# 32 bytes more per buffer: the start addresses of weights, xs and h spread over 256 bytes

## The chip, the cores and the metric

The kernel runs on one core of a Trainium2 chip, in one launch. The metric is the device time of that core in microseconds (us), from the first to the last instruction. TensorE (PE in the profile) multiplies, VectorE (DVE), ScalarE (ACT) and GpSimd (POOL) do the elementwise work, SyncE (SP) issues the loads.

## The reference, cut to what matters

Two macaron layers over 512 tokens of width 1024. Each layer is a half-weighted SwiGLU feed-forward, a mixer, and a second feed-forward; a final RMSNorm follows.

```python
def swiglu(x, w_gate, w_up, w_down):
    return (jax.nn.silu(x @ w_gate) * (x @ w_up)) @ w_down

for i in range(DEPTH):                      # DEPTH = 2, D_FF = 2816
    x = x + 0.5 * swiglu(rms_norm(x, ffn_norm[i, 0]), ...)
    hx = rms_norm(x, mix_norm[i])
    x = x + (mixer_ab(hx, ...) if i % 2 == 0 else mixer_cd(hx, ...))
    x = x + 0.5 * swiglu(rms_norm(x, ffn_norm[i, 1]), ...)
return rms_norm(x, final_norm)
```

`mixer_ab` is attention (global beside neighbourhood), `mixer_cd` is a pair of gated convolutions. Everything is float32.

## The kernel before

Activations lie transposed, features on partitions and the 512 tokens along the free axis: `x` is 8 chunks of 128x512. To keep float32 precision with TensorE's fp32r type, each operand is split into a high part (rounded to fp32r) and a low part (the rest), and each product is made as three matmuls (`mm3`, lines 97 to 99): high weights by high x, high weights by low x, low weights by high x. In each of them the weights (128x128) are the stationary operand, loaded by a weight load of its own (PEld in the profile), and x (128x512) is the moving one, streamed through.

The tiles that these matmuls read, all 128 partitions high:

- `raw`: weights as they come from DRAM, 1024 columns, 3 buffers.
- `wh` and `wl`: high and low weights, 512 columns (four blocks of 128), made from `raw` by `split` (lines 117 and 118: a cast on ScalarE, a subtraction on VectorE or GpSimd), 5 buffers each, used in turn. Such a pair is a *piece*; it serves four chunks of the contraction, 12 matmuls. In `mixer_cd` every other piece comes from a second pool, `wx` (`self.extra`), with 5 more buffers each.
- `xs`: the gained high and low part of a chunk of x, side by side, 2x512 columns, 8 buffers, made by `absorb` (lines 126 and 127). It is the moving operand of gate, up and most projections.
- `h`: high and low part of a chunk of the hidden layer, 2x512 columns, 22 buffers in a pool of each feed-forward, made by `gate`. It is the moving operand of the down product.

The mixers' own moving tiles (`y`, `yc`, `yd`, and attention's) are other tiles with buffers of their own.

A feed-forward runs 22 chunks of gate and up (8 chunks of xs each, sums in PSUM tile `psg`), then 8 chunks of down (22 chunks of h each, sums in `psd`). Pieces are made three ahead of their use by `feed`, which `piece` calls. The order of the instructions on each engine is set by the framework's scheduler from the program's order, and in the mixers for PE by hand.

Of the kernel before, what the change touches and what calls it, by code (L numbers as in the profile page):

```python
# [10 lines left out]
F32R = mybir.dt.float32r  # L11
# [5 lines left out]
P = 128  # L17
D = 1024
T = 512
# [8 lines left out]
class Trunk:  # L28
# [27 lines left out]

# [1 line left out]
    def plan(self, units):  # L58
# [16 lines left out]
    def feed(self, upto):  # L75
        nc = self.nc
        while len(self.ready) < min(upto + 1, len(self.pieces)):
            i, c0, c1 = self.pieces[len(self.ready)]
            self.load(i + 1)
            w, r = c1 - c0, self.loaded[i][:, c0:c1]  # L80
            ph, pl = self.wh, self.wl
            if self.extra and len(self.ready) < self.extra_end and len(self.ready) % 2:
                ph = pl = self.extra
            h = ph.tile([P, 512], F32R, tag="wh", name=self.name("wh"))[:, :w]
            l = pl.tile([P, 512], F32R, tag="wl", name=self.name("wl"))[:, :w]
            self.split(h, l, r, self.nc.gpsimd if self.share and len(self.ready) % self.share == 0 else None)
            self.ready.append((h, l))
# [13 lines left out]
    def chunk(self, ps, xs, first=True, last=True):  # L101
        """ps += W[chunk].T @ x over the contraction pieces xs; yields after each."""
        n = len(xs)
        for k, x in enumerate(xs):
            if k % 4 == 0:
                h, l = self.piece()
            s = slice(k % 4 * P, (k % 4 + 1) * P)
            self.mm3(ps, h[:, s], l[:, s], x[:, 0], x[:, 1], first and k == 0, last and k == n - 1)
            yield
# [4 lines left out]

# [1 line left out]
    def split(self, hi, lo, src, eng=None):  # L116
# [3 lines left out]
    def absorb(self, k, gain):  # L120
        """From the residual chunk k: its gained (high, low) pair."""
        nc = self.nc
        g = self.par[:, gain + k : gain + k + 1]
        x = self.x[k]
        xs = self.xsp.tile([P, 2, T], F32R, tag="xs", name=self.name("xs"))
        nc.scalar.activation(xs[:, 0], x, AF.Copy, scale=g)  # L126
        nc.vector.scalar_tensor_tensor(xs[:, 1], x, g, xs[:, 0].bitcast(F32), op0=ALU.mult, op1=ALU.subtract)  # L127
        self.xs[k] = xs
# [11 lines left out]
    def table(self, func, after):  # L140
        """Loads ScalarE's table of func once `after` is there."""
        self.nc.scalar.activation(self.warm, after, func, bias=self.eps)

    def root(self, y, src, scale, after, v=None):
        """y = (src * scale + eps) ** -0.5; then the table of `after`."""
        nc = self.nc
        n = src.shape[1]
        e, v, a = self.t(n), v if v is not None else self.t(n), self.t(n)
        nc.scalar.activation(e, src, AF.Abs_reciprocal_sqrt, bias=self.eps, scale=scale)
        nc.vector.tensor_scalar(v, src, scale, EPS, op0=ALU.mult, op1=ALU.add)  # L150
        if after is not None:
            self.table(after, e[:, :1])
        nc.vector.tensor_tensor(a, e, e, op=ALU.mult)
        nc.vector.scalar_tensor_tensor(a, a, -0.5, v, op0=ALU.mult, op1=ALU.mult)
        nc.vector.scalar_tensor_tensor(y, a, 1.5, e, op0=ALU.add, op1=ALU.mult)  # L155

    def norm(self, after=None):
        """rB[:, t] = rsqrt(mean of x[t]^2 + eps) on all partitions."""
        nc = self.nc
        s = self.fr.tile([P, 2, T], F32R, tag="fr", name=self.name("ss"))  # L160
        self.split(s[:, 0], s[:, 1], self.S)
        ps = self.ps("m")
        nc.tensor.matmul(ps, lhsT=self.ones, rhs=s[:, 0], start=True, stop=False)
        nc.tensor.matmul(ps, lhsT=self.ones, rhs=s[:, 1], start=False, stop=True)
        self.rB = self.rbp.tile([P, T], F32, tag="rB", name=self.name("rB"))
        self.root(self.rB, ps, 1.0 / D, after)
# [13 lines left out]

# [1 line left out]
    def ffn(self, gain, natural=False, start=False):  # L182
# [41 lines left out]
    def gate(self, hp, pg, pu):  # L224
        nc = self.nc
        g, s, h = self.t(), self.t(), self.t()
        nc.vector.tensor_tensor(g, pg, self.rB, op=ALU.mult)  # L227
        nc.scalar.activation(s, g, AF.Silu)  # L228
        nc.vector.tensor_tensor(s, s, self.rB, op=ALU.mult)  # L229
        nc.vector.tensor_tensor(h, pu, s, op=ALU.mult)  # L230
        hh = hp.tile([P, 2, T], F32R, tag="h", name=self.name("h"))
        self.split(hh[:, 0], hh[:, 1], h)
        return hh

    def finish(self, hs):
        """The last down projection and the final norm; the last chunk by halves of the tokens."""
        nc = self.nc
        gf = lambda k: self.par[:, 48 + k : 49 + k]
        for d in range(NK - 1):
            ps = self.ps("d")  # L240
# [6 lines left out]
        pieces = []  # L247
# [53 lines left out]

# [1 line left out]
    def column(self, k, n=1):  # L303
        return self.par[:, k : k + n]

    def rope(self, src):
        """src [feature pairs on partitions, tokens] -> rotated, in place of a new tile."""
        nc = self.nc
# [65 lines left out]
    def row_scales(self):  # L374
        """Per token, on its partition: r, and for each head of A the scale of its scores."""
        nc = self.nc
        ps = self.ps("m")
        for t in range(4):
            nc.tensor.transpose(ps[:, t * P : (t + 1) * P], self.rB[:, t * P : (t + 1) * P], self.ident)
        self.rc = self.abc.tile([P, 4], F32, tag="rc", name="rc")  # L380
        nc.vector.tensor_copy(self.rc, ps.rearrange("p (t q) -> p t q", q=P)[:, :, 0])
# [23 lines left out]
    def values(self, half):  # L405
        """Value columns of `half`, tokens on partitions; yields after each contraction step."""
        nc = self.nc
# [60 lines left out]
    def fill(self, n):  # L468
        """n steps of the fillers; those of A's output wait for its heads."""
        done = 0  # L470
# [6 lines left out]

    # units: (kind, pair, e, tile); "a": 128 queries x 512 keys, "b": 128 queries x 256 keys
    def scores(self, u):
# [41 lines left out]
    def turn(self, u, pr):  # L521
        """Probabilities of a unit to keys-on-partitions, split into the group's tiles."""
        nc = self.nc
# [14 lines left out]
    def mix(self, u, pt):  # L538
        """Values by a finished group's probabilities. The values' high and low parts stand side
        by side, so each pass leaves two sums, one of them on the head's own partitions."""  # L540
        nc = self.nc
# [29 lines left out]

    def ab_start(self):
        """Keys, queries and first values, their small chains a step behind the products."""
        nc = self.nc

# [102 lines left out]

# [1 line left out]
    def padded(self):  # L680
# [6 lines left out]
    def conv_vector(self, j, u, k0=0):  # L687
        """Taps k0.. of 31 over the padded chunk u on VectorE, one per step, the sums in PSUM;
        alone, with two sums in turn, else in turn with the next chunk."""
        nc = self.nc  # L690
# [19 lines left out]
    def conv_spare(self, j, u, k1=31):  # L710
        """Taps ..k1 on ScalarE (products) and GpSimd (sums)."""
        nc = self.nc
# [21 lines left out]
    def conv_step(self, n):  # L734
        """n steps of the convs on VectorE: the first alone, the others two at a time."""
        while n > 0 and self.convs:
# [7 lines left out]
    def total(self, src):  # L744
        """Sum of src over the partitions, on all of them, in PSUM."""
        ps = self.ps("m")
# [63 lines left out]
    def c_out(self):  # L810
        """The short conv's half of the output product; six of its sums stay open in PSUM."""
        nc = self.nc
# [40 lines left out]
    def mixer_cd(self, gain):  # L853
        nc = self.nc
        with self.tc.tile_pool(name="cdp", bufs=1) as self.cdp, self.tc.tile_pool(name="wx", bufs=5) as self.extra:
# [22 lines left out]
            with self.tc.manual_schedule(engines={mybir.EngineType.PE}):  # L878
# [5 lines left out]
                self.share = 0  # L884
                # the first sums side by side: the chunks of y come one by one
                k = 3
# [63 lines left out]
def cols(v):  # L950
    """[..., n * 128] -> [128, ... * n]"""
    return v.reshape(-1, P).T


def bias_table(rpb):
    """[head, query in tile, tile, key]: the bias of each pair in reach, -1e30 elsewhere.
    Tokens run down the grid's columns: token = col * 8 + row."""
    q = np.arange(512).reshape(4, P, 1)
# [9 lines left out]
def constants():  # L968
    """identity, blocks of ones by head, signed swap of pairs, head selectors, cos, sin."""
    f = np.float32  # L970
# [57 lines left out]
```

## Time and profile before

| what | value |
|---|---|
| device time, median of 2 runs | 1896.6 us (1895.97 and 1897.22) |
| profiled execution, span | 1896.4 us |
| PE busy | 1862.0 us, 98% |
| weight loads (PEld) busy | 1525.5 us, 80% |
| VectorE, ScalarE, GpSimd busy | 51%, 40%, 20% |
| HBM traffic | 94 GB/s over the span |
| TensorE's mean granted clock | 0.992 of full speed |

The profiled execution's own time is its span; the two timed runs lie 0.4 us below and 0.8 us above it, so nothing has to be added around it. A matmul's duration in the profile runs from its start to its modelled end and overlaps the next one's, so what it costs in a stream is read from the distance between the starts of two matmuls that follow each other, here called the *interval*.

### The profile page before, as it was taken

How to read it: one execution, taken by the hardware profiler on the slowest of the kernel's cores; microseconds unless marked ns; L12 is line 12 of the kernel's file. 1: busy time of each engine (PE TensorE's matmuls, PEld its weight loads, DVE VectorE, ACT ScalarE, POOL GpSimd, SP SyncE). 2: the span in 40 equal slices, each digit the busy share in tenths (PEclk: the TensorE clock that was granted, in tenths of full speed). 3: DMA queues.
4: the chain of work that ended last, by engine and by line, in shares of the span. 5: the costliest groups of instructions: out<-in, count | busy, mean ns of one | idle time of the engine just before them, and what ended most of it. 6: DMA issues, size and time to landing. Idle time of an engine off the chain costs nothing.

```text
span 1896.4 us, 22618 instructions
## 1 busy us (share of the span) xinstructions
PE 1862.0 (98%) x8382; PEld 1525.5 (80%) x8382; DVE 973.7 (51%) x1534; ACT 764.3 (40%) x1336; POOL 381.0 (20%) x358
## 2 busy tenths in 40 slices
PE   8999999989999999999999999999998999999997
PEld 7888888878877888888888888888886788888886
DVE  6544433387865744443334444422599755444333
ACT  5333333357755533333333333333464543333332
POOL 0000000045332222222222222222399100000000
PEclk9999999999999999999999999999999899999999
DMA  4232233312122323223323222233322222222332
GB/s 169 100 100 93 95 92 97 118 55 91 40 95 67 125 97 100 98 90 92 93 95 102 98 100 100 86 98 96 122 90 67 87 82 99 100 97 90 92 96 71
DMA packets 56576, 179.00 MB, mean 94 GB/s; under 512 B 6161, under 2 KB 8465, under 8 KB 56465
## 3 DMA queue, kind: packets, MB, share of 16 engines
q1 hardware_dynamic: 55888, 176.71, 28.8%
q8 instruction: 66, 1.08, 0.2%
q10 hardware_dynamic: 576, 0.84, 0.1%
q14 instruction: 46, 0.37, 0.1%
HBM read 175.43 MB, written 2.10 MB: 94 GB/s over the span
## 4 chain that ended last, share of the span: by engine, by line
PE 95%; DVE 3%; issue 1%; ACT 0%; POOL 0%; DMA 0%; DVEq 0%; POOLq 0%; ACTq 0%
PE psg L97 20%; PE psg L98 20%; PE psg L99 19%; PE psd L97 11%; PE psd L98 11%; PE psd L99 11%; PE psm L528 1%; PE psg L558 1%; PE psg L557 1%; PE psg L489 0%; PE psg L490 0%; DVE psm L700 0%; DVE wl L118 0%; DVE x L280 0%; DMA raw<-in_gate 0%
## 5 line engine op out<-in xcount | busy, mean ns | idle before, releaser
L117 ACT CAST wh<-raw 128x512 fp32r<-128x512 f32 (+1 forms) x662 | 400.2, 607 | 905.1 <-PE psg L98 549.8
L97 PE MATMUL psg<-xs,wh 128*128 128x512 f32 x1592 | 619.6, 390 | 6.1 <-ACT xs L126 6.1
L98 PE MATMUL psg<-xs,wh 128*128 128x512 f32 x1592 | 620.6, 390 | 0.0
L99 PE MATMUL psg<-xs,wl 128*128 128x512 f32 x1592 | 620.1, 390 | 0.0
L118 DVE TENSOR_TENSOR wl<-raw,wh 128x512 fp32r<-128x512 f32 (+1 forms) x469 | 326.7, 697 | 454.5 <-ACT wh L117 451.4
L118 POOL TENSOR_TENSOR wl<-raw,wh 128x512 fp32r<-128x512 f32 (+1 forms) x193 | 250.8, 1300 | 634.4 <-ACT wh L117 624.2
L97 PEld LDWEIGHTS psg<-xs,wh 128*128 128x128 f32 x1592 | 299.5, 188 | 69.0 <-ACT xs L126 6.1
L98 PEld LDWEIGHTS psg<-xs,wh 128*128 128x128 f32 x1592 | 299.4, 188 | 62.6 <-DVE xs L127 0.5
L99 PEld LDWEIGHTS psg<-xs,wl 128*128 128x128 f32 x1592 | 299.4, 188 | 62.4
L99 PE MATMUL psd<-h,wl 128*128 128x512 f32 (+1 forms) x726 | 282.0, 388 | 0.0
L98 PE MATMUL psd<-h,wh 128*128 128x512 f32 (+1 forms) x726 | 282.0, 388 | 0.0
L97 PE MATMUL psd<-h,wh 128*128 128x512 f32 (+1 forms) x726 | 281.8, 388 | 0.0
L99 PEld LDWEIGHTS psd<-h,wl 128*128 128x128 f32 x726 | 136.3, 188 | 31.2
L97 PEld LDWEIGHTS psd<-h,wh 128*128 128x128 f32 x726 | 136.3, 188 | 31.2
L98 PEld LDWEIGHTS psd<-h,wh 128*128 128x128 f32 x726 | 136.3, 188 | 31.1
L230 DVE TENSOR_TENSOR t<-psg,t 128x512 f32<-128x512 f32 x87 | 60.1, 691 | 124.4 <-PE psg L99 124.1
L227 DVE TENSOR_TENSOR t<-psg,rB 128x512 f32<-128x512 f32 x87 | 60.1, 691 | 121.4 <-PE psg L99 121.4
L229 DVE TENSOR_TENSOR t<-t,rB 128x512 f32<-128x512 f32 x88 | 72.7, 826 | 34.4 <-ACT t L228 30.7
L118 DVE TENSOR_TENSOR h<-t,h 128x512 fp32r<-128x512 f32 x88 | 73.0, 830 | 32.5 <-ACT h L117 28.8
L280 POOL TENSOR_TENSOR x<-x,t 128x256 f32<-128x256 f32 x4 | 3.2, 829 | 396.3 <-DVE t L155 396.3
L626 POOL MEMSET pb<- 128x384 f32 x2 | 0.8, 418 | 371.3 <-PE psd L99 371.3
L228 ACT ACTIVATE t<-t 128x512 f32<-128x512 f32 x88 | 55.6, 632 | 25.9 <-DVE t L227 25.8
(238 smaller groups left out, 1635.3 us busy)
## 6 DMA issues: line engine op xcount, KB each, us to landing
raw<-in_gate SPq DMA_DIRECT2D x84, 512.0 KB, 3.2
raw<-in_up SPq DMA_DIRECT2D x84, 512.0 KB, 3.2
raw<-in_down SPq DMA_DIRECT2D x64, 448.0 KB, 3.3
raw<-in_down SPq DMA_DIRECT2D x32, 512.0 KB, 3.5
raw<-in_cdin SPq DMA_DIRECT2D x18, 512.0 KB, 3.2
raw<-in_abqk SPq DMA_DIRECT2D x13, 512.0 KB, 3.3
raw<-in_about SPq DMA_DIRECT2D x16, 256.0 KB, 2.7
bias<-in_bias SPq DMA_DIRECT2D x8, 512.0 KB, 3.3
```

The source lines that it names most:

```text
L97: mm(ps, lhsT=aH, rhs=bH, start=first, stop=False)
L98: mm(ps, lhsT=aH, rhs=bL, start=False, stop=False)
L99: mm(ps, lhsT=aL, rhs=bH, start=False, stop=last)
L117: self.nc.scalar.copy(hi, src)
L118: (eng or self.nc.vector).tensor_tensor(lo, src, hi.bitcast(F32), op=ALU.subtract)
L227: nc.vector.tensor_tensor(g, pg, self.rB, op=ALU.mult)
L228: nc.scalar.activation(s, g, AF.Silu)
L229: nc.vector.tensor_tensor(s, s, self.rB, op=ALU.mult)
L230: nc.vector.tensor_tensor(h, pu, s, op=ALU.mult)
L528: nc.tensor.transpose(ps[:, i * P : (i + 1) * P], pr[:, i * P : (i + 1) * P], self.ident)
L557: nc.tensor.matmul(ps, lhsT=w, rhs=pt[0][:, p0:p1], start=first, stop=False)
L558: nc.tensor.matmul(ps, lhsT=w, rhs=pt[1][:, p0:p1], start=False, stop=last)
```

## The change

Three kinds of tile get 8 float32 columns (32 bytes) more per partition than they use: `wh` and `wl` (both pools), `xs`, and `h`. The views that the instructions use stay as they were. The diff also empties comments and docstrings (lines stay where they are); its core:

```diff
@@ feed
-            h = ph.tile([P, 512], F32R, tag="wh", name=self.name("wh"))[:, :w]
-            l = pl.tile([P, 512], F32R, tag="wl", name=self.name("wl"))[:, :w]
+            h = ph.tile([P, 520], F32R, tag="wh", name=self.name("wh"))[:, :w]
+            l = pl.tile([P, 520], F32R, tag="wl", name=self.name("wl"))[:, :w]
@@ absorb
-        xs = self.xsp.tile([P, 2, T], F32R, tag="xs", name=self.name("xs"))
+        xs = self.xsp.tile([P, 2 * T + 8], F32R, tag="xs", name=self.name("xs"))[:, : 2 * T].rearrange("p (a t) -> p a t", a=2)
@@ gate
-        hh = hp.tile([P, 2, T], F32R, tag="h", name=self.name("h"))
+        hh = hp.tile([P, 2 * T + 8], F32R, tag="h", name=self.name("h"))[:, : 2 * T].rearrange("p (a t) -> p a t", a=2)
```

On all five engines the instructions stand in the same order before and after, with the same buffers and the same waits; only addresses differ. The start of each buffer within a partition, modulo 256 bytes, as the two programs allocate them (a block of weights begins a multiple of 512 bytes into its buffer, a low part 2048 bytes into its own, so these offsets hold for every operand that a matmul reads):

| buffers | before | after, in the order of the buffers |
|---|---|---|
| `xs` (8) | 128 | 128, 160, 192, 224, 0, 32, 64, 96 |
| `wh` (5) | 128 | 128, 160, 192, 224, 0 |
| `wl` (5) | 128 | 32, 64, 96, 128, 160 |
| `wh` in `wx` (5) | 64 | 128, 160, 192, 224, 0 |
| `wl` in `wx` (5) | 64 | 32, 64, 96, 128, 160 |
| `h` (22) | 0 | 64, 96, 128, ... in steps of 32 |
| `raw` (3) | 128 | 128 |
| `t`, `S`, `rB` | 128 | 192 |
| `y` of attention | 0 | 64 |
| `yc`, `yd` of the convolutions (split) | 64 | 128 |

Below, the *distance* of a matmul is the start of its moving operand less the start of the weights that are loaded while it runs (those of the next matmul), modulo 256 bytes.

## Rows read from the trace of the kernel before

**Rows 1.** Page, parts 1 and 2: busy time, and the span in 40 slices.
```profile
PE 1862.0 (98%) x8382; PEld 1525.5 (80%) x8382; DVE 973.7 (51%) x1534; ACT 764.3 (40%) x1336; POOL 381.0 (20%) x358
...
PE   8999999989999999999999999999998999999997
...
PEclk9999999999999999999999999999999899999999
```

**Rows 2.** Page, part 4: the chain that ended last, by engine and line.
```profile
PE 95%; DVE 3%; issue 1%; ACT 0%; POOL 0%; DMA 0%; DVEq 0%; POOLq 0%; ACTq 0%
PE psg L97 20%; PE psg L98 20%; PE psg L99 19%; PE psd L97 11%; PE psd L98 11%; PE psd L99 11%; PE psm L528 1%; PE psg L558 1%; PE psg L557 1%; PE psg L489 0%; PE psg L490 0%; DVE psm L700 0%; DVE wl L118 0%; DVE x L280 0%; DMA raw<-in_gate 0%
```

**Rows 3.** Groups by line and shape: matmuls of line 97.
```profile
L97 PE MATMUL psg<-xs,wh 128*128 128x512 f32 x1592 | 619.6, 390 | 6.1 <-ACT xs L126 6.1
...
L97 PE MATMUL psd<-h,wh 128*128 128x512 f32 x682 | 269.4, 395 | 0.0
...
L97 PE MATMUL psd<-xs,wh 128*128 128x512 f32 x80 | 35.1, 438 | 1.7 <-DVE t L433 1.7
```

**Rows 4.** Timeline of PE, gate and up: start, duration, then engine and operation.
```profile
1604.75 0.39 PE L98 MATMUL psg<-xs,wh 128*128 128x512 f32 x1
1604.97 0.39 PE L99 MATMUL psg<-xs,wl 128*128 128x512 f32 x1
...
1649.17 0.39 PE L99 MATMUL psg<-xs,wl 128*128 128x512 f32 x1
```

**Rows 5.** Timeline of PE, a down product.
```profile
1802.70 0.40 PE L99 MATMUL psd<-h,wl 128*128 128x512 f32 x1
1802.94 0.39 PE L97 MATMUL psd<-h,wh 128*128 128x512 f32 x1
...
1848.43 0.40 PE L97 MATMUL psd<-h,wh 128*128 128x512 f32 x1
```

**Rows 6.** Timeline of PE, output product of the convolutions.
```profile
1490.54 0.39 PE L97 MATMUL psg<-yc,wh 128*128 128x512 f32 x1
...
1492.58 0.40 PE L97 MATMUL psd<-yc,wh 128*128 128x512 f32 x1
1492.82 0.39 PE L98 MATMUL psd<-yc,wh 128*128 128x512 f32 x1
...
1495.15 0.39 PE L99 MATMUL psd<-yc,wl 128*128 128x512 f32 x1
...
1496.30 0.40 PE L98 MATMUL psd<-yc,wh 128*128 128x512 f32 x1
...
1496.77 0.39 PE L97 MATMUL psd<-yc,wh 128*128 128x512 f32 x1
...
1498.13 0.40 PE L97 MATMUL psg<-yd,wh 128*128 128x512 f32 x1
```

**Rows 7.** Timeline of PE, input projection of the convolutions, one piece from `wx`.
```profile
1408.72 0.39 PE L97 MATMUL psg<-xs,wh 128*128 128x512 f32 x1
...
1411.47 0.39 PE L97 MATMUL psg<-xs,wh 128*128 128x512 f32 x1
```

**Rows 8.** Stretches: bounds, length, busy PE, PEld, DVE, ACT, POOL, granted clock, DMA.
```profile
640.00:870.00 230.00, 230.00 (x1015) 190.34 (x1015) 102.39 (x132) 80.80 (x130) 54.30 (x42) 1.00 0.29 96
...
260.00:360.00 100.00, 100.00 (x430) 80.43 (x430) 38.26 (x59) 31.43 (x53) 0.00 (x0) 1.00 0.33 97
```

**Rows 9.** Waits of the weight split: total us, times, longest.
```profile
ACT wh L117 <- PE psg L98: 549.8, 339, 3.9
DVE wl L118 <- ACT wh L117: 451.4, 298, 5.2
```

**Rows 10.** Cast of the weights (min/median/max ns): in the convolutions, then in gate and up.
```profile
L117 ACT CAST wh<-raw x16: 600/604/622, 1389.6 to 1437.3; 128x512 fp32r<-128x512 f32 x16
...
L117 ACT CAST wh<-raw x52: 621/622/622, 1599.8 to 1738.5; 128x512 fp32r<-128x512 f32 x52
```

**Rows 11.** Page, part 5: all casts of weights.
```profile
L117 ACT CAST wh<-raw 128x512 fp32r<-128x512 f32 (+1 forms) x662 | 400.2, 607 | 905.1 <-PE psg L98 549.8
```

## The prediction

> **What bounds the kernel now.** I read the page first: PE is busy for 98% of the span and at 9 tenths or more in 36 of 40 slices [rows 1], and the chain of waits that ended last is 95% PE, almost all of it the three matmuls of `mm3` [rows 2]. So the time is a count of matmuls times their interval, and a change that moves no instruction can act only through that interval, or through a slower split that comes late. The groups give the counts: 1592 matmuls of each of the three lines with xs into `psg`, 80 of each with xs into `psd`, 682 of each with h at full width [rows 3]. That is 3 x 1672 = 5016 intervals behind xs and 3 x 682 = 2046 behind h.
>
> The timeline gives the intervals. In gate and up, 196 of them lie between the first and the last row shown: (1649.17 - 1604.75) / 196 = 226.6 ns [rows 4]. In down, again 196: (1848.43 - 1802.70) / 196 = 233.3 ns [rows 5]. [...] What the table of addresses says of them: xs and its weights both begin at 128 modulo 256 (distance 0), h begins at 0 and its weights at 128 (distance 128).
>
> Whether the address is what counts is told by a place where it changes and the moving tile doesn't. In the output product of the convolutions every other piece comes from `wx`, so yc (at 64) meets weights at 64 for 12 matmuls and then weights at 128 for 12. With weights at 64 (distance 0), 9 intervals from 1490.54 to 1492.58: 2.04 / 9 = 226.7 ns. With weights at 128 (distance 192), 11 from 1492.58 to 1495.15: 2.57 / 11 = 233.6 ns. Back at 64, 6 from 1496.77 to 1498.13: 1.36 / 6 = 226.7 ns [rows 6]. The PSUM tile isn't the cause, since the last two of these are both `psd`. One more distance: xs at 128 with weights at 64 (distance 64), 12 intervals from 1408.72 to 1411.47, 2.75 / 12 = 229.2 ns [rows 7]. So the price by distance is 226.7 (0), 229.2 (64), 233.3 (128), 233.6 (192).
>
> **The change, part by part.** *xs and its weights.* Today nearly all of these sit at distance 0, the cheapest of the four that the trace shows. Eight places for xs against five for `wh` and five for `wl` put about an eighth of the intervals at each of the eight distances 0, 32, ..., 224. The odd multiples of 32 don't occur before; I take them as lying among their neighbours, so the mean by distance is (226.7 + 229.2 + 233.3 + 233.6) / 4 = 230.7 ns. There is a second part: after a change of distance the stream takes a few matmuls to settle. After the step back to distance 0 the 5 intervals from 1495.15 to 1496.30 take 1.15 / 5 = 230 ns, before 226.7 is reached [rows 6]. With the change the distance moves at almost every matmul, between `wh` and `wl` and from one chunk to the next, so the stream never settles; against that, a single matmul at a dear distance may not reach its full price either. I add 0.8, between nothing and the 3.3 seen: 231.5 ns. The cost is 5016 x (231.5 - 226.7) = 24.1 us, and none of it is hidden, as PE has no gap there to give.
>
> *h and its weights.* They leave distance 128 for the same mixture: 2046 x (231.5 - 233.3) = -3.7 us.
>
> *Bounds of both.* From below, every interval comes to 226.7: nothing for xs, -6.6 x 2046 = -13.5 us for h. From above, every interval is as long as the longest single step of the alternating stretches, 0.24 us between neighbouring rows against a mean of 0.2333 [rows 5, 6]; taken as 237 ns that is 10.3 x 5016 + 3.7 x 2046 = 59 us. I take 231.5 because it is nearest to the mixture of rows, and both ends go into the range.
>
> *y, yc, yd and attention's tiles.* Their own length doesn't change, but their weights now spread, and yc and yd met two distances in turn before. Some 400 matmuls, at 226.7 to 233.6 before and in the same span after: 0, with 400 x 6.9 = 2.8 us either way.
>
> *The split and the other elementwise work.* Its instructions write to starts that are multiples of 32 instead of 64 or 128. The nearest row is the cast in the convolutions, where half of the outputs start at 64 and half at 128: 600 to 622 ns, against 621 to 622 with all of them at 128 [rows 10]. No loss shows. ScalarE's cast waited 549.8 us in all for PE to free a buffer, and VectorE another 451.4 us for the cast [rows 9], so a split that grew by a few per cent would stay under that cover; if all of it showed on PE, 2% of the 400.2 us of all casts of weights [rows 11] would be 8 us. I take 0. The buffers' count, the loads and their sizes are unchanged.
>
> **The sum.** +24.1 - 3.7 = +20.4 us on the profiled execution's own 1896.4, which is within 0.2 us of the median of the runs: **1917 us**, 1.1% slower. That is under the 2% that a measurement of this kernel can tell from no change.
>
> **The rivals.** *Nothing happens: 1896 us.* The address would have to stand in for something else, say the second pool's place high in SBUF or the h pool's. For it: the h stretch and the gate stretch differ in more than the address, and the convolutions' rows are short. Against it: yc reads at 226.7 from `wx`, high in SBUF, and at 233.6 from the ordinary pool, while xs does the opposite, 229.2 and 226.7 [rows 4, 6, 7]. No fixed price of a pool gives both; a distance does.
> [...]
>
> *Faster: the 226.7 is itself a collision.* [...] If two streams that begin in the same place of every 256 bytes are what costs this, then spreading them apart removes some of it wherever the distance isn't 0. [...] It decides from a mean of (5016 x 226.7 + 2046 x 233.3) / 7062 = 228.6 ns downwards, in effect when some of the four unseen distances are much cheaper than the seen ones. Against it: distances 64, 128 and 192 are all dearer than 0. A mild form, in which the mixture comes to no more than 226.7, gives 1896.4 - 13.5 = 1883 us.
> [...]
>
> *Clearly slower: the stream never settles.* If the settling rather than the distance is what costs, and every change of distance brings the long step of an alternating pair without the short one, the mean comes to 235 ns: 8.3 x 5016 + 1.7 x 2046 = 45 us, 1942 us. It passes the 2% line (1934.5 us) from a mean of 234.0 ns on, 5.4 above 228.6. For it: the distance changes at nearly every matmul after the change. Against it: in the rows the long step is always followed by a short one.
>
> **How the numbers follow.** The forecast (mean interval 229.5 to 233.5, 1903 to 1931 us) gets 0.56; nothing happens, 0.10; faster, 0.14, two thirds of it in the mild form near 1883 and 0.05 below 1858.7 us (2%); the stream never settles, 0.20, of which 0.14 lies above 1934.5 us. The range, 1889 to 1942 us, leaves out the strong form of the faster rival, part of the mild one and the upper end of the slow one, together about 2 in 10. From the same cases: faster by over 2% 0.05, within 2% 0.81, slower by over 2% 0.14.
>
> **What would show it.** In the profile after, the mean interval of a stretch of gate and up should be near 231.5 ns instead of 226.6, with no period, and that of a down product about the same instead of 233.3; the two products should have become alike. PE's busy share and the chain should stay as they are, and the granted clock at 1.00. The forecast is wrong if gate and up keep 226.6 (the address isn't it), if both fall under 228.6 (the faster rival), or if they go to 235 and above; and wrong in its reason if PE shows gaps behind the weight split, since then an elementwise engine and not the interval made the difference.

## The result, and the profile after

The changed kernel takes 1916.66 us (1915.64 and 1917.69) against 1896.6 before: a ratio of 1.0105, 95% interval 1.0086 to 1.0125, so 0.9 to 1.3% slower. The profiled execution is the one of 1915.64 us; its span is 1913.9, so about 1.7 us lie outside the span. Every run here of which both are recorded takes 1.7 to 1.9 us longer than its span, those of the kernel before included (1891.77 and 1889.9 us, for one). The span of 1896.4 before should therefore not be read as that execution's time, as "Time and profile before" has it; by these runs it took about 1898 us, an estimate. From span to span the change costs 17.5 us, from median to median 20.1.

The page after, parts 1, 2 and 4, answers to [rows 1] and [rows 2]:

```profile
PE 1882.2 (98%) x8382; PEld 1525.1 (80%) x8382; DVE 970.3 (51%) x1534; ACT 764.2 (40%) x1336; POOL 381.4 (20%) x358
...
PE   8999999999999999999999999999999999999997
...
PEclk9999999999999999999999999999999999999999
...
PE 96%; DVE 3%; issue 1%; ACT 0%; POOL 0%; DMA 0%; DVEq 0%; SPq 0%; POOLq 0%; ACTq 0%
```

The same instructions, the same share of PE, nearly the same mean clock (0.992 and 0.993); weight loads, ScalarE and GpSimd are as busy as before to within 0.4 us, VectorE 3.4 us less. Only PE's busy time has grown, by 20.2 us. Nothing waits anew: the matmuls themselves come further apart. The timeline of PE in the kernel after, first in gate and up, then in a down product, answers to [rows 4] and [rows 5]; in each, 196 intervals lie between the first and the last row shown:

```profile
699.78 0.39 PE L99 MATMUL psg<-xs,wl 128*128 128x512 f32 x1
...
745.21 0.40 PE L97 MATMUL psg<-xs,wh 128*128 128x512 f32 x1
```

```profile
289.63 0.40 PE L97 MATMUL psd<-h,wh 128*128 128x512 f32 x1
...
335.14 0.39 PE L98 MATMUL psd<-h,wh 128*128 128x512 f32 x1
```

Gate and up: (745.21 - 699.78) / 196 = 231.8 ns, before 226.6. Down: (335.14 - 289.63) / 196 = 232.2 ns, before 233.3. The two products have become alike.

Neither the granted clock nor a gap set the two products apart before. [rows 8] show 1.00 and a PE that is busy all the time, in other stretches of the same two products. For the stretches that the prediction read, the view says the same (length, busy PE, then the other engines, granted clock, DMA), gate and up first:

```profile
1604.75:1649.17 44.42, 44.42 (x197) 36.79 (x196) 21.42 (x33) 15.38 (x25) 0.00 (x0) 1.00 0.28 95
1802.70:1848.43 45.73, 45.73 (x197) 36.79 (x196) 15.05 (x25) 14.61 (x24) 0.00 (x0) 1.00 0.33 94
```

and for the two stretches of the kernel after:

```profile
699.78:745.21 45.43, 45.43 (x198) 36.80 (x196) 19.54 (x25) 15.14 (x25) 10.39 (x8) 1.00 0.28 93
289.63:335.14 45.51, 45.51 (x198) 36.81 (x196) 17.51 (x27) 14.27 (x24) 0.00 (x0) 1.00 0.33 95
```

Where the 17.5 us lie is told by the matmul of each norm (line 163), which stands once in every sublayer. Its starts in the timeline of PE, kernel before:

```profile
25.82 0.39 PE L163 MATMUL psm<-ss,ones 128*128 128x512 f32 x1
377.50 0.39 PE L163 MATMUL psm<-ss,ones 128*128 128x512 f32 x1
635.75 0.39 PE L163 MATMUL psm<-ss,ones 128*128 128x512 f32 x1
998.77 0.39 PE L163 MATMUL psm<-ss,ones 128*128 128x512 f32 x1
1361.82 0.39 PE L163 MATMUL psm<-ss,ones 128*128 128x512 f32 x1
1532.89 0.39 PE L163 MATMUL psm<-ss,ones 128*128 128x512 f32 x1
```

The same rows, kernel after:

```profile
25.28 0.39 PE L163 MATMUL psm<-ss,ones 128*128 128x512 f32 x1
381.50 0.40 PE L163 MATMUL psm<-ss,ones 128*128 128x512 f32 x1
640.41 0.40 PE L163 MATMUL psm<-ss,ones 128*128 128x512 f32 x1
1008.21 0.40 PE L163 MATMUL psm<-ss,ones 128*128 128x512 f32 x1
1376.09 0.39 PE L163 MATMUL psm<-ss,ones 128*128 128x512 f32 x1
1545.71 0.40 PE L163 MATMUL psm<-ss,ones 128*128 128x512 f32 x1
```

Differences of neighbouring rows, before and after: first feed-forward 351.7 and 356.2, attention 258.25 and 258.91, second feed-forward 363.0 and 367.8, third 363.1 and 367.9, convolutions 171.1 and 169.6, and the last feed-forward up to the end of the span 363.5 and 368.2. The four feed-forwards lose 4.5, 4.8, 4.8 and 4.7 us, 18.8 together. That is what the intervals give: 1056 matmuls with xs and 528 with h in one of them (at full width 462 in the last), 1056 x 5.2 - 528 x 1.1 = 4.9. The convolutions, whose 480 matmuls with xs should have lost about 2 us (252 x 5.2, and 228 with weights from `wx`, which had 229.2 before [rows 7], x 2.6), are 1.5 us shorter. What PE waited for there, from 1390 to 1530 us (total, times, longest), kernel before:

```profile
PE psd L97 <- ACT yc L117: 5.6, 3, 3.4
PE psd L98 <- DVE yc L118: 2.8, 2, 1.6
```

and kernel after:

```profile
PE psd L97 <- ACT yc L117: 4.1, 2, 3.4
PE psd L98 <- DVE yc L118: 1.6, 1, 1.6
```

PE waits for the elementwise chain that makes yc, 2.7 us less than before. Two things lie in this. The stage up to the place where the granted clock falls, and the stretch that it then stays at 0.50, kernel before:

```profile
1361.82:1465.83 104.01, 100.94 (x441) 82.34 (x439) 102.41 (x132) 59.15 (x95) 89.64 (x68) 1.00 0.26 86
1465.83:1479.48 13.65, 8.32 (x17) 5.50 (x18) 8.57 (x12) 2.90 (x5) 3.75 (x3) 0.50 0.30 97
```

and kernel after:

```profile
1376.09:1480.73 104.64, 102.58 (x441) 82.45 (x439) 100.57 (x133) 59.30 (x95) 90.33 (x68) 1.00 0.27 88
1480.73:1490.97 10.24, 6.63 (x13) 4.20 (x14) 6.89 (x11) 2.89 (x5) 2.55 (x2) 0.50 0.26 89
```

Up to the fall PE works 1.6 us more and idles 1.0 us less: there the slower matmuls do lie partly under the work on yc. The rest is the stretch at a granted clock of 0.50, 3.4 us shorter with 1.7 us less of idle PE in it, against 1.3 us more from there to the end of the stage (53.4 and 54.7 us). The shorter stretch at 0.50 need not come from the slower matmuls: xs_256_longer below, with the intervals of the kernel before, has 10.24 us of it too, and 169.2 us for this stage. Why it differs between executions is not shown.

### The profile page after: what moved, and what is told of

The parts are those of the page before. It is cut to its first block, busy times and chain, and to the rows that moved or that the text cites. A ratio compares the mean times of both kernels' runs of the same rounds, so it can differ in the third digit from the quotient of the medians.

```text
span 1913.9 us, 22618 instructions
## 1 busy us (share of the span) xinstructions
PE 1882.2 (98%) x8382; PEld 1525.1 (80%) x8382; DVE 970.3 (51%) x1534; ACT 764.2 (40%) x1336; POOL 381.4 (20%) x358
## 4 chain that ended last, share of the span: by engine, by line
PE 96%; DVE 3%; issue 1%; ACT 0%; POOL 0%; DMA 0%; DVEq 0%; SPq 0%; POOLq 0%; ACTq 0%
PE psg L97 20%; PE psg L98 20%; PE psg L99 20%; PE psd L97 11%; PE psd L99 11%; PE psd L98 11%; PE psm L528 1%; PE psg L558 1%; PE psg L557 1%; PE psg L489 0%; PE psg L490 0%; DVE psm L700 0%; DVE wl L118 0%; DVE x L280 0%; DMA x<-in_x 0%
## 5 line engine op out<-in xcount | busy, mean ns | idle before, releaser
L97 PE MATMUL psg<-xs,wh 128*128 128x512 f32 x1592 | 626.5, 394 | 6.4 <-ACT xs L126 6.4
L98 PE MATMUL psg<-xs,wh 128*128 128x512 f32 x1592 | 628.2, 395 | 0.0
L99 PE MATMUL psg<-xs,wl 128*128 128x512 f32 x1592 | 627.3, 394 | 0.0
L118 DVE TENSOR_TENSOR h<-t,h 128x512 fp32r<-128x512 f32 x88 | 73.0, 830 | 32.7 <-ACT h L117 28.9
```

The costliest lines, as they stand in the source:

```text
L97: mm(ps, lhsT=aH, rhs=bH, start=first, stop=False)
L98: mm(ps, lhsT=aH, rhs=bL, start=False, stop=False)
L99: mm(ps, lhsT=aL, rhs=bH, start=False, stop=last)
L118: (eng or self.nc.vector).tensor_tensor(lo, src, hi.bitcast(F32), op=ALU.subtract)
```

## The experiments

The theory: the interval is set by the *distance*, as defined with the change, and 0 is the cheap one; spreading the starts took gate and up away from it. Rivals: the moving tile's own start, the tile's length or place, and, in the other direction, an unseen distance cheaper than 0. All intervals below are read as above: 196 intervals, from about 700 us in gate and up and from about 290 us in down. None of these kernels leaves out or moves an instruction; all have the same waits, and only addresses differ. Inserted lines move the three matmuls to lines 98 to 100 or 99 to 101.

**h brought to distance 0 (h_zero).** Nothing is longer; 128 unused bytes stand ahead of the pools that are opened stage by stage, so the mixers' own tiles and `wx` move too.

```diff
+        pool("gap2", 1).tile([P, 32], F32, tag="gap2", name="gap2")
         self.psum = pool("psum", 1, space=bass.MemoryType.PSUM)
```

> No tile is longer; 128 unused bytes stand ahead of the stage pools, so h begins at 128 like its weights. Distance theory: down falls from 233.3 to 226.7 ns an interval, 2046 x -6.6 = -13.5 us, 1883 us. Rival that the interval belongs to the h pool or to the down product itself: 1896 to 1897 us.

Measured: 1881.31 us (1877.97 to 1882.72), ratio 0.9915, 95% interval 0.9899 to 0.9932. The timeline of its down product:

```profile
289.82 0.39 PE L98 MATMUL psd<-h,wh 128*128 128x512 f32 x1
...
334.25 0.39 PE L99 MATMUL psd<-h,wh 128*128 128x512 f32 x1
```

(334.25 - 289.82) / 196 = 226.7 ns, from 233.3. The same instructions, tiles and lengths, 128 bytes further on: the down product isn't slow by itself, and neither is its pool. In the profile the four feed-forwards, in which only h has moved, take 13.3 us less together (3.5, 3.5, 3.4 and 2.9), where 2046 intervals were to give 13.5. This is faster than both kernels of the comparison.

**One part at a time (weights_only, xs_only, h_only).** Each of the three diffs of the change alone.

> Only the weight buffers are 32 bytes longer; xs stays at 128, h at 0. Distance theory: gate and up go to about 232 ns, down to about 232, 1896.4 + 5016 x 5.3 - 2046 x 1.3 = 1920 us. Rival that the moving operand's own start sets the interval: both intervals as before, 1896 us.

> Only xs is longer; weights stay at 128, so the distance is constant over the three matmuls of a chunk and changes from chunk to chunk. If the settled prices hold (226.7, 229.2, 233.3, 233.6 at 0, 64, 128, 192): 230.7 ns, 1916 us. If the stream needs longer than three matmuls to settle: about 232 ns, 1923 us. Down stays at 233.3.

> Only h is longer. Gate and up stay at 226.6; down goes to 230.7 (settled prices, -5 us, 1891 us) or to about 232 (unsettled, -2.7 us, 1894 us). Rival that longer tiles cost by themselves: down slower than 233.3, over 1896 us.

Measured, one run each beside a median of 1896.64 for the kernel before: weights_only 1915.59 us, intervals 232.0 (gate and up) and 231.1 (down); xs_only 1919.66 us, 232.5 and 232.3; h_only 1895.41 us, 226.7 and 232.6. With xs left at 128 and only its weights spread, gate and up slow down as much as after the whole change, so the moving operand's own start isn't what counts. Either side alone costs nearly everything, and the parts don't add: once one of the two is spread, spreading the other changes little. h_only shows that a longer h costs nothing by itself and that a spread gains 0.7 ns on distance 128 (232.6 for 233.3). Two misses: the down product of xs_only was to stay at 233.3 and has 232.3, at the same constant distance of 128; and that of weights_only, at 231.1, is lower than forecast. Its expectation has h at 0, but ten weight buffers that are each 32 bytes longer stand ahead of h and move it by 320, to 64. The timeline of xs_only's down product:

```profile
289.70 0.40 PE L98 MATMUL psd<-h,wh 128*128 128x512 f32 x1
...
335.24 0.40 PE L99 MATMUL psd<-h,wl 128*128 128x512 f32 x1
```

**The constant distances (six kernels).** Tiles of the old lengths; gaps of n and m float32 columns ahead of the weights and ahead of the stage pools hold xs and h each at one distance, two prices per kernel. Each was run once.

```diff
+        pool("gap1", 1).tile([P, n], F32, tag="gap1", name="gap1")
         self.raw = pool("raw", 3)
...
+        pool("gap2", 1).tile([P, m], F32, tag="gap2", name="gap2")
         self.psum = pool("psum", 1, space=bass.MemoryType.PSUM)
```

n and m are 56 and 56 (d32_h96), 40 and 8 (d96_h160), 24 and 24 (d160_h224), 8 and 40 (d224_h32), 48 and 16 (d64_h192), 64 and 96 (d256_h256).

> Tiles of the old lengths; unused bytes ahead of the weights and of the stage pools put xs at a constant distance of 32 from its weights and h at a constant 96. Steady distances, never seen before. If the price rises smoothly from 0: xs about 228 ns, h about 231. If an odd multiple of 32 is cheaper (the collision rival): under 226.7. If only distance 0 is cheap: both about 233.

> Constant distances: xs 96, h 160. The price must belong to the distance and not to the tile: xs at 96 here equals h at 96 in the run before, within 0.5 ns. By interpolation 231 and 233 ns.

> Constant distances: xs 160, h 224. xs at 160 equals h at 160 of the run before. By interpolation 233 and 230 ns; under 226.7 only by the collision rival.

> Constant distances: xs 224, h 32. Each equals the other tile's price at the same distance in the earlier runs. If the settled prices at all eight distances average near 230.7 and the changed kernel has 232, the rest is the settling.

> Constant distances: xs 64, h 192, the two that the kernel before shows only over 12 matmuls at a time. If every distance but 0 costs the same once it is constant: both near 233.3 ns, about 1926 us. If the short stretches gave the steady price: xs 229.2, h 233.6, 1909 us.

> Constant distance of 256 bytes modulo 512 for xs and h. If the pattern repeats every 256 bytes: both 226.7 ns, 1881 to 1884 us, as with distance 0. If it repeats at 512 or more: both near 233.3 ns, 1930 us.

| kernel | time, us | distance of xs: interval, ns | distance of h: interval, ns |
|---|---|---|---|
| before | 1896.6 | 0: 226.6 | 128: 233.3 |
| d32_h96 | 1924.34 | 32: 233.3 | 96: 233.3 |
| d96_h160 | 1926.46 | 96: 233.4 | 160: 234.3 |
| d160_h224 | 1928.21 | 160: 234.3 | 224: 233.4 |
| d224_h32 | 1924.62 | 224: 233.3 | 32: 233.4 |
| d64_h192 | 1903.51 | 64: 228.9 | 192: 233.4 |
| d256_h256 | 1882.87 | 256: 226.7 | 256: 226.7 |

The rows behind three of these, gate and up each, in the order d32_h96, d160_h224, d64_h192:

```profile
699.62 0.40 PE L99 MATMUL psg<-xs,wh 128*128 128x512 f32 x1
...
745.35 0.40 PE L100 MATMUL psg<-xs,wh 128*128 128x512 f32 x1
```

```profile
699.68 0.39 PE L99 MATMUL psg<-xs,wh 128*128 128x512 f32 x1
...
745.60 0.40 PE L100 MATMUL psg<-xs,wh 128*128 128x512 f32 x1
```

```profile
699.80 0.39 PE L101 MATMUL psg<-xs,wl 128*128 128x512 f32 x1
...
744.66 0.39 PE L99 MATMUL psg<-xs,wh 128*128 128x512 f32 x1
```

Where a distance was held by both tiles (32, 96, 160, 224), the prices agree to 0.1 ns: the distance carries the price, not the tile. The pattern repeats at 256 bytes, since 256 costs what 0 costs, 226.7 ns. No distance that was tried is cheaper than 0, which ends the rival that a collision at 0 could be spread away. And all distances but 0 and 64 are about equally dear: there is no slope between 0 and 128 on which 32 would lie, and d32_h96 missed its smooth alternative of 228 by 5 ns. d64_h192 gives 228.9 and 233.4 ns for the 229.2 and 233.6 of [rows 6] and [rows 7]: stretches of 12 matmuls had told the steady price.

**Longer, but by 256 bytes (xs_256_longer).** In `absorb`, before's `[P, 2, T]` becomes `[P, 2 * T + 64]`, with the same view of it as in the change.

```diff
-        xs = self.xsp.tile([P, 2, T], ...)
+        xs = self.xsp.tile([P, 2 * T + 64], ...)[:, : 2 * T].rearrange("p (a t) -> p a t", a=2)
```

> xs is 256 bytes longer instead of 32, so its buffers are moved as much or more but still begin at 128 modulo 256. Distance theory: 226.6 in gate and up, 233.3 in down, 1896 us. Rival that a longer tile with a gap costs by itself: gate and up near 232, 1923 us.

Measured: 1891.86 us beside before's 1894.74 to 1899.1, intervals 226.7 and 233.4, as before. Length and gap cost nothing; the start modulo 256 does. This single run lies under those of before that stand beside it, but not under all: beside h_zero, one run of the kernel before took 1891.77 us. The profile says where the difference lies: the four feed-forwards take the same 351.7, 363.0, 363.1 and 363.5 us as before, and attention 254.3 instead of 258.3, with the granted clock at 1.00 over the stage instead of 0.98. Attention in the kernel before:

```profile
377.50:635.75 258.25, 248.91 (x1311) 203.37 (x1310) 192.87 (x429) 162.09 (x354) 99.63 (x122) 0.98 0.23 76
```

and in xs_256_longer:

```profile
376.99:631.26 254.27, 244.91 (x1312) 199.58 (x1310) 192.03 (x429) 161.96 (x354) 100.92 (x122) 1.00 0.23 77
```

**Distance 0 in the convolutions too (all_zero).** h_zero, and `cu` (a tile of the convolutions) is given 576 columns instead of 514, so that the pools behind it begin at 128 as well.

```diff
-        u = self.cdp.tile([P, 514], F32, tag="cu", name=self.name("cu"), bufs=2)
+        u = self.cdp.tile([P, 576], F32, tag="cu", name=self.name("cu"), bufs=2)
```

> As the run with h at distance 0, and the convolutions' tiles also moved, so that the second weight pool, yc and yd begin at 128 too: distance 0 everywhere but in attention. 229 intervals of xs by 6 ns and some 90 of yc and yd by 2 to 3: 1.5 to 2 us less than that run's 1881.3, about 1879.5 us; the difference to it is too small for the measurement, so the intervals decide.

Measured: 1882.43 us (1882.15 to 1882.88), ratio 0.9927, 95% interval 0.9911 to 0.9944; no better than h_zero. The intervals, which the expectation names as the judge, did fall. Twelve matmuls with xs and weights from `wx` in h_zero, at distance 192,

```profile
1407.98 0.40 PE L98 MATMUL psg<-xs,wh 128*128 128x512 f32 x1
...
1410.78 0.39 PE L98 MATMUL psg<-xs,wh 128*128 128x512 f32 x1
```

and in all_zero, at 0:

```profile
1406.08 0.39 PE L98 MATMUL psg<-xs,wh 128*128 128x512 f32 x1
...
1408.80 0.39 PE L98 MATMUL psg<-xs,wh 128*128 128x512 f32 x1
```

That is 2.80 / 12 = 233.3 and 2.72 / 12 = 226.7 ns, 1.5 us over 228 such intervals. The norm's matmul at both ends of the convolutions, in h_zero

```profile
1349.33 0.39 PE L164 MATMUL psm<-ss,ones 128*128 128x512 f32 x1
1518.59 0.39 PE L164 MATMUL psm<-ss,ones 128*128 128x512 f32 x1
```

and in all_zero:

```profile
1348.50 0.39 PE L164 MATMUL psm<-ss,ones 128*128 128x512 f32 x1
1519.78 0.39 PE L164 MATMUL psm<-ss,ones 128*128 128x512 f32 x1
```

169.3 and 171.3 us: this stage, the only one that the longer `cu` changes, became 2.0 us longer. The stretch at a granted clock of 0.50 in it, h_zero:

```profile
1454.32:1464.56 10.24, 6.27 (x12) 3.89 (x13) 7.26 (x11) 2.90 (x5) 2.54 (x2) 0.50 0.29 98
```

and all_zero:

```profile
1449.95:1467.02 17.07, 10.16 (x20) 6.11 (x21) 12.15 (x17) 4.55 (x8) 7.36 (x6) 0.50 0.27 93
```

The granted clock is at 0.50 for 6.8 us more (17.07 for 10.24), and PE waits 8.9 us for yc instead of 6.8. So the 1.5 us that the matmuls gave are outweighed; what comes first, the wait or the clock, is not shown. The chain of waits (shares from 1340 to 1480 us, h_zero) has much besides PE in this stage:

```profile
by line: POOL yd L721 24.0%; issue 11.6%; PE psg L99 10.9%; PE psg L100 10.8%; PE psg L98 10.8%; POOL wl L119 7.1%; DVE psm L701 5.1%; DVE wl L119 2.7%; DVE yc L119 2.0%; PE psd L98 1.8%; PE psd L99 1.8%; POOL cc L798 1.4%; PE psd L100 1.4%
```

GpSimd's sum of the convolution is the longest single line there, and PE's lines together have 37.5%. The forecast of 1.5 to 2 us less counted matmuls where they only partly set the end.

## Why the prediction came out right, point by point

*That the interval counts and the address sets it* was right. PE's share and the chain stayed as they were, the instructions too, the clock in both products as well, and the two products became alike, at 231.8 and 232.2 ns for 231.5. h_zero is the clean proof, as 128 bytes of nothing move 2046 intervals by 6.6 ns, which makes 13.5 us (13.3 in the profile's feed-forwards), and the time from 1896.6 to 1881.3, where 1883 was expected.

*The price by distance* had a wrong middle. The step "I take them as lying among their neighbours" put the four unseen distances at a mean of 230.7 with the seen ones; held constant, they cost 233.3, 233.4, 234.3 and 233.3. The mean of the eight constant prices is (226.7 + 233.3 + 228.9 + 233.4 + 233.3 + 234.3 + 233.4 + 233.3) / 8 = 232.1 ns.

*The settling* was the second wrong step, the other way. I added 0.8 ns for a stream that never settles; against 232.1 the changed kernel's 231.8 and 232.2 leave nothing to add. A mean taken 1.4 ns too low and an addition 0.8 ns too high partly cancelled in 231.5, which is luck. The reading behind the addition was also short: in [rows 6] the stream is back at 226.7 only from 1496.77 on, 7 intervals after 1495.15, which average 1.62 / 7 = 231 ns. That the mixture costs the mean of the constant prices must not be read as each matmul paying its own price: taking all starts of full-width matmuls with xs from the trace after and sorting the intervals under 300 ns by distance, the 613 at distance 0 average 231.0 and the 608 at distance 160 average 231.5, though constant they cost 226.7 and 234.3. In a mixture the price is one of the mixture, 231.1 to 232.6 ns in the four kernels that have one. Nor is the mean of the constant prices exact: for the down product of weights_only, h at 64 and the weights at their ten places, it would be 232.5 ns, and 231.1 was measured.

*The sum.* xs: 5016 x (231.8 - 226.6) = +26.1 us where +24.1 was forecast. h: 2046 x (232.2 - 233.3) = -2.3 where -3.7 was forecast. That is 23.8, and the span grew by 17.5. (5016 at 226.6 is itself a little too much, since 228 of them were at distance 64.) "None of it is hidden" failed in the convolutions, where 480 of the 5016 intervals lie: up to the fall of the clock 1.0 of 1.6 us was taken back by less idle time of PE, which waits for yc there. The stretch at a granted clock of 0.50, 3.4 us shorter, did the rest, and the stage became 1.5 us shorter instead of about 2 longer; of the clock in that stage the prediction has no term. Attention, whose 312 matmuls with xs should have lost 1.6 us, lost 0.7. The start of the kernel was 0.5 us earlier. So 1917 for 1916.66 is closer than the reasoning was: from span to span +20.4 was forecast and 17.5 came, and the 1.8 us between span and time, taken as 0, lie the other way. The constant distances show the same shortfall: the span of d160_h224 should be 5016 x 7.7 + 2046 x 0.1 = 39 us longer than before and is 30.0 longer: 31.2 in the feed-forwards (32.7 by their intervals), and 1.2 less in the mixers and at the start.

*The rivals.* "Nothing happens" is ruled out by the interval itself: 226.7 against 233.3 ns in h_zero and the kernel before, with the same tiles, the same count and nothing changed for h but its start. Why a different start costs 6.6 ns is not shown. "Faster" is ruled out at the steps of 32 bytes that were tried, none of which is under 226.6. No run shows its strong form, which the range leaves out and which has 0.05 below 1858.7 us: the shortest run of all took 1877.97 us (h_zero). "The stream never settles" at 235 isn't seen: the mixtures stay under 233.

*The split* cost nothing, as taken: with starts at multiples of 32 the cast of the weights runs at 602/604/621 ns (min, median, max) in the convolutions, for 600/604/622 in [rows 10].

## What to carry to other kernels

When a stream of matmuls has no gaps, compare the interval between starts in stages of the same shape; a difference of 3% at the same clock and width (here 233.3 against 226.7 ns) can be the start addresses of moving and stationary operand. Here they should agree modulo 256 bytes, which a few unused bytes ahead of a pool bring about, and which a tile length that isn't a multiple of 256 bytes undoes for most of the buffers. Before spreading addresses against an assumed collision, look for the places where the kernel already has two distances: the prices are in the trace. Here stretches of 12 matmuls gave the steady price to 0.3 ns (229.2 and 233.6 for 228.9 and 233.4), while the first matmuls after a change of distance did not (230 and 231 ns on the way back to 226.7), and distances that weren't seen should not be interpolated. When a sum of intervals and the time disagree, compare the stages one by one, their granted clock included: here xs_256_longer and the kernel before, with the same intervals, differ by 4.0 us in attention and 1.9 in the convolutions, where the slower matmuls should have cost 1.6 and about 2.

## What the runs showed of the hardware that was not expected

Equal starts are the cheap case: 226.7 ns with the two operands at the same place modulo 256 bytes, 233.3 to 234.3 at six of the seven other multiples of 32, and 228.9 at 64. The step from 0 to those six is 6.6 to 7.6 ns a matmul, about 3%.

A constant distance doesn't always give one price: at 128, the down product takes 233.3 ns in the kernel before and 232.3 in xs_only, where the same tiles lie 256 bytes further on; in xs_256_longer, where they lie 2048 bytes further on, it takes 233.4.

What stays open: why 0 is cheap and 64 lies between; why 128 has two prices; what the stream does in a mixture, whose price is known only as a mean; whether it is the weights loaded during a matmul or its own that count, since in the kernels with constant distances both have the same start; and steps finer than 32 bytes, which were not tried. The distance as cause is shown; a mechanism behind it is not.
